# Up projections of a gated feed-forward layer, four tiles at a time, with seven products of token halves for half of the contraction

## The chip, the cores and the metric

The kernel runs on one core of one Trainium2 chip, as one program. The metric is device time of one execution in microseconds (us), the median over several executions. The engines are named as the profile names them: PE is TensorE (PEld its weight loads, which can run under matmuls), DVE is VectorE, ACT is ScalarE, POOL is GpSimd, SP is SyncE, which here issues most of the DMA transfers.

## The reference

Two trunk layers of a diffusion backbone run over 512 latent tokens of width 1024. Each has a mixer (attention and a gated recurrence in the first, a short gated convolution in the second) and then a gated convolutional feed-forward part. All data are float32. The change lies in the feed-forward part and in the computation of the modulation vectors (`mod`), which runs beside it:

```python
D_MODEL, SEQ, DEPTH, D_FF = 1024, 512, 2, 2816

def conv_ffn(h, w_up, conv_w, conv_b, w_down):
    a, val = jnp.split(h @ w_up, 2, axis=-1)
    return (jax.nn.gelu(dwconv3(a, conv_w, conv_b), approximate=False) * val) @ w_down

for layer in range(DEPTH):
    mod = silu_c @ ada_w[layer] + ada_b[layer]
    ...                                   # the mixer of the layer, x = x + gate_m * y
    h = modulate(rms_norm(x, norm_ffn_w[layer]), shift_f, scale_f)
    x = x + gate_f[:, None, :] * conv_ffn(h, ffn_w_up[layer], ffn_conv_w[layer],
                                          ffn_conv_b[layer], ffn_w_down[layer])
```

## The kernel before

Every float32 operand of a large product is split into a hi part in TensorE's rounded format and a lo part that holds the rest, and a product is three matmuls: hi·hi, hi·lo and lo·hi (`mm3`, L246 to L248). Activations lie with features on the 128 partitions and the 512 tokens along a row. So `h` is eight tiles of 128x512 (`src[k]`, a hi and a lo part each, named `hf`), and the up projection makes 44 output tiles of 128x512: 22 for `a` and 22 for `val`.

The class `Weights` feeds the products. A raw tile (`wraw`, two buffers of 1 MB) is loaded by a DMA that SP issues (L59). `conv` makes the hi part of 1024 columns on ACT (L84, `whi`) and the lo part on DVE (L85, `wlo`). Each has three buffers, so a new hi part waits until the matmuls that read the third last one are done.

`ffn_up` goes through eleven steps. Step 0 is `quad`: four tiles at once in two halves of 256 tokens, since the second half of `h` is still being normalised while the first is used (`rest`). Steps 1 to 10 are a pair of `a` tiles (`pair`: two tiles, eight parts of the contraction, three matmuls each, 48 matmuls of 512 columns), then a pair of `val` tiles. Here the two pairs are called a group. Behind a pair the convolution over tokens (`conv3`: one ACT instruction L1079, two DVE instructions L1080 and L1081), the gelu (L1108), the product with `val` (L1116) and the split of the result (L242 on ACT, L243 on DVE) follow, straight out of PSUM. PSUM has six banks for such results (`acc_t`), each of 512 columns.

`units` runs pieces of `mod` between products: one piece is a load of 256 KB (`ar`) and one DVE instruction (L462), and every eighth piece adds some more and a small matmul (`pad`). Before the change layer 0's up projection has 20 pieces, its down projection (`project_back` of `d0`) four per step, and the mixer of layer 1 two per call.

The framework that builds the program takes the instructions of each engine from the code and puts them into an order of its own. Engines run their own instructions in that order and wait for one another by semaphores.

## Time and profile before

| what | before |
|---|---|
| median of three runs (lowest to highest) | 1344.23 us (1342.78 to 1346.13) |
| the profiled execution | 1343.25 us |
| its span, first to last instruction | 1341.5 us |
| granted TensorE clock, mean over the span | 0.999 |
| busy share of PE, DVE, ACT, POOL | 98%, 61%, 39%, 6% |
| HBM traffic | 165.21 MB read, 2.10 MB written |

The profiled execution is 1.75 us longer than its span, and 0.98 us shorter than the median. A busy share is a mean over all stages of the kernel; what one stage is bound by is read from its own stretch.

### The profile page before, as it was taken

To read this page: it belongs to the slowest core of one execution; us is meant where nothing else is said; L and a number is where in the kernel's file an instruction comes from. 1 tells how busy PE (TensorE), PEld (TensorE's weight loads), DVE (VectorE), ACT (ScalarE), POOL (GpSimd) and SP (SyncE) were. 2 spreads that over 40 slices of the span, in tenths; PEclk is the share of its full clock that TensorE was granted. 3 is DMA by queue.
4 is the path that set the end of the run, shared out by engine and by line. 5 is a ranking of instruction groups with operands and counts; after the bars stand their busy time and mean duration, and the time that the engine had idled before them with its cause. 6 is when DMAs were issued, how large, how long until landed. Compare 5 with 4: busy or idle time off the path is not lost. (4 is left out here: it accounts for less than half of the span.)

```text
span 1341.5 us, 19127 instructions
## 1 busy us (share of the span) xinstructions
PE 1318.2 (98%) x7736; PEld 1126.1 (84%) x7736; DVE 821.3 (61%) x1354; ACT 527.9 (39%) x815; POOL 84.4 (6%) x87
## 2 busy tenths in 40 slices
...
GB/s 290 266 125 80 32 32 85 149 188 132 151 196 95 118 118 118 118 118 126 123 205 196 206 95 141 141 144 168 128 95 120 97 100 103 101 99 73 88 110 63
DMA packets 170825, 172.21 MB, mean 128 GB/s; under 512 B 14321, under 2 KB 144753, under 8 KB 170737
## 3 DMA queue, kind: packets, MB, share of 16 engines
...
q8 instruction: 60, 0.98, 0.3%
q14 instruction: 29, 0.23, 0.1%
HBM read 165.21 MB, written 2.10 MB: 125 GB/s over the span
## 5 line engine op out<-in xcount | busy, mean ns | idle before, releaser
L84 ACT CAST whi<-wraw 128x1024 fp32r<-128x1024 f32 (+1 forms) x202 | 207.7, 1031 | 469.2 <-PE ppv L247 93.4
L85 DVE TENSOR_TENSOR wlo<-wraw,whi 128x1024 fp32r<-128x1024 f32 (+1 forms) x202 | 243.5, 1207 | 217.8 <-ACT whi L84 216.5
L247 PE MATMUL ppa<-hf,whi 128*128 128x512 f32 (+1 forms) x448 | 161.6, 361 | 0.0
L246 PE MATMUL ppa<-hf,whi 128*128 128x512 f32 (+1 forms) x448 | 161.2, 360 | 0.0
L248 PE MATMUL ppa<-hf,wlo 128*128 128x512 f32 (+1 forms) x448 | 160.2, 358 | 0.0
L247 PE MATMUL ppv<-hf,whi 128*128 128x512 f32 x320 | 126.1, 394 | 0.0
L246 PE MATMUL ppv<-hf,whi 128*128 128x512 f32 x320 | 125.8, 393 | 0.0
L248 PE MATMUL ppv<-hf,wlo 128*128 128x512 f32 x320 | 124.3, 388 | 0.0
L462 DVE SCALAR_TENSOR_TENSOR aa<-ar,sil,aa 128x512 f32<-128x512 f32 x140 | 105.4, 753 | 17.4 <-DMA ar<-in_ada_w_dram 15.9
L1205 PE MATMUL pd<-whi,g 128*128 128x256 f32 x352 | 98.1, 279 | 0.0
L1207 PE MATMUL pd<-wlo,g 128*128 128x256 f32 x352 | 98.0, 278 | 0.0
L1206 PE MATMUL pd<-whi,g 128*128 128x256 f32 x352 | 97.7, 278 | 0.0
L246 PEld LDWEIGHTS ppa<-hf,whi 128*128 128x128 f32 x448 | 84.1, 188 | 13.9
L248 PEld LDWEIGHTS ppa<-hf,wlo 128*128 128x128 f32 x448 | 84.1, 188 | 13.2
L247 PEld LDWEIGHTS ppa<-hf,whi 128*128 128x128 f32 x448 | 84.2, 188 | 12.2
L1116 DVE TENSOR_TENSOR ppv<-ppv,cv 128x512 f32<-128x512 f32 x40 | 28.0, 700 | 86.0 <-PE ppv L248 86.0
L246 PE MATMUL pbd<-g,whi 128*128 128x512 f32 (+1 forms) x192 | 72.3, 377 | 0.0
L247 PE MATMUL pbd<-g,whi 128*128 128x512 f32 (+1 forms) x192 | 72.0, 375 | 0.0
L248 PE MATMUL pbd<-g,wlo 128*128 128x512 f32 (+1 forms) x192 | 71.7, 373 | 0.0
L246 PEld LDWEIGHTS ppv<-hf,whi 128*128 128x128 f32 x320 | 60.1, 188 | 13.8
L248 PEld LDWEIGHTS ppv<-hf,wlo 128*128 128x128 f32 x320 | 60.1, 188 | 13.4
L247 PEld LDWEIGHTS ppv<-hf,whi 128*128 128x128 f32 x320 | 60.2, 188 | 11.9
...
## 6 DMA issues: line engine op xcount, KB each, us to landing
wraw<-in_ffn_w_up_dram SPq DMA_DIRECT2D x44, 1024.0 KB, 5.1
ar<-in_ada_w_dram SPq DMA_DIRECT2D x160, 256.0 KB, 2.9
wraw<-in_ffn_w_down_dram SPq DMA_DIRECT2D x16, 1024.0 KB, 5.1
wraw<-in_od_w_in_dram SPq DMA_DIRECT2D x12, 1024.0 KB, 5.3
...
wraw<-in_ev_w_out_dram SPq DMA_DIRECT2D x4, 1024.0 KB, 7.3
```

The costliest lines, as they stand in the source:

```text
L84: self.nc.scalar.copy(hv, rv)
L85: self.pin(self.nc.vector.tensor_tensor(lv, rv, hv.bitcast(F32), ALU.subtract))
L246: TE.matmul(o, wh, mh, start=start, stop=False, skip_group_check=True)
L247: TE.matmul(o, wh, ml, start=False, stop=False, skip_group_check=True)
L248: TE.matmul(o, wl, mh, start=False, stop=stop, skip_group_check=True)
L462: pin(V.scalar_tensor_tensor(self.acc[:], raw[:], sil[:, r, 0:1], self.acc[:], ALU.mult, ALU.add))
L1116: V.tensor_tensor(ov[i][:], ov[i][:], t[i][:], ALU.mult)
L1205: TE.matmul(o[i][:, 0:256], gh[:, ts], w[0][:, k - k0], start=k == 0, stop=False)
L1206: TE.matmul(o[i][:, 0:256], gl[:, ts], w[0][:, k - k0], start=False, stop=False)
L1207: TE.matmul(o[i][:, 0:256], gh[:, ts], w[1][:, k - k0], start=False, stop=k == FT - 1)
```

## The change

The up projection's steps 1 to 10 become ten calls of `group`, which makes four tiles at once: two of `a` and two of `val`, in four PSUM banks. The contraction is cut in two. The second half (`k` 4 to 7) is done as before in matmuls of 512 columns (blocks `W1` for the first `a` and `val` tile, `W2` for the second). The first half (`k` 0 to 3) is a product of a 2x2 arrangement of weight blocks with a 2x2 arrangement of inputs (two halves of `k`, two halves of the tokens) by seven products instead of eight, each of 12 matmuls of 256 columns. Its weight blocks are `A11`, `A12`, `A22` and the sums `S1` to `S4`, made by four DVE instructions of 512 columns per group (`_block`); its inputs are quarters of `h` and the differences `T1` to `T4`, made once per layer (`differences`), behind the quad's normalisation. `T1` overwrites a part of `h` that nobody needs after the quad. Partial products that go into more than one output are copied out of PSUM by ACT (eight copies of 256 columns per group) and added by DVE (four of 256, two of 512); the convolution and the rest then read SBUF. The weights come from a new array `upq` in the order of use, two tiles of 1 MB per group as before. The pieces of `mod` leave layer 0's up projection for its down projection (five per step) and for the mixer of layer 1 (three per call); layer 1's up projection has two calls per group for nine groups. The line numbers of the changed code are higher by 4 to some 160: its matmuls are L288 to L290, its hi and lo parts L125 and L126, its copies L1176, its adds L1181 and L1201.

```diff
+QORDER = ["S1", "A11", "A12", "W1", "S2", "S3", "S4", "A22", "W2"]
...
+        nm = self.plan[c][1][s]
+        while self.nload <= min(c + 1 + (nm == "W2"), len(self.plan) - 1):
             self._load()
+        if isinstance(nm, str):
+            self._block(c, nm)
+            return
...
+    HOME = {"S1": ("a", 0), "A11": ("a", 1), "A12": ("b", 0), "W1": ("c", None), "S2": ("d", 0), "S3": ("d", 1),
+            "S4": ("e", 0), "A22": ("e", 1), "W2": ("f", None)}
+    def _block(self, c, nm):
+        V = self.nc.vector
+        quarters = self.raw[c][0]
+        A21, A22, A11, A12 = (quarters[:, 0, 512 * i : 512 * i + 512] for i in range(4))
+        if nm == "S1":
+            s3 = self.pool.tile([P, 512], F32, tag="ws3", name=f"ws3{self.nsub}", bufs=1)
+            V.tensor_tensor(s3[:], A11, A21, ALU.subtract)
+            self.half["S3"] = s3[:]
+            V.tensor_tensor(A21, A21, A22, ALU.add)
+        elif nm == "S2":
+            V.tensor_tensor(A21, A21, A11, ALU.subtract)
+        elif nm == "S4":
+            V.tensor_tensor(A21, A12, A21, ALU.subtract)
+        if nm in ("W1", "W2"):
+            at = 1024 * (nm == "W2")
+            src = self.raw[c + 1][0][:, 0, at : at + 1024]
+        else:
+            src = {"A11": A11, "A12": A12, "A22": A22, "S3": self.half.get("S3")}.get(nm, A21)
+        key, z = self.HOME[nm]
+        if z in (None, 0):
+            self.half[key] = [self.pool.tile([P, 1024], F32R, tag=t, name=f"{t}{self.nsub}", bufs=3) for t in ("whi", "wlo")]
+        at = 512 * (z or 0)
+        hi, lo = (t[:, at : at + src.shape[-1]] for t in self.half[key])
+        self.nc.scalar.copy(hi, src)
+        V.tensor_tensor(lo, src, hi.bitcast(F32), ALU.subtract)
+        self.ready.append(tuple(t.rearrange("p (g k c) -> p g k c", g=2, c=P) for t in (hi, lo)))
+        self.nsub += 1
...
     def ffn_up_plan(l):
-        r = []
-        for j in range(FT // 2):
-            r += cols(up[l], 256 * j) + cols(up[l], FF + 256 * j)
+        r = cols(up[l], 0) + cols(up[l], FF)
+        for j in range(FT // 2 - 1):
+            q = [a["upq"][l, j, i][:, None, :] for i in range(2)]
+            r += [([q[0]], QORDER), ([q[1]], [])]
         return r
...
-                units(4)
+                units(4 if len(groups) == 1 else 5)
...
-    def quad(nm, src, rest):
+    def quad(nm, src, rest, done=lambda: None):
...
+        done()
...
+    def differences(l, src):
+        A, B = HALF
+        h = []
+        for k in range(4):
+            t = gp.tile([P, T], F32, tag=f"g{k}", name=f"hs{l}{k}")
+            V.tensor_tensor(t[:], src[k][0].bitcast(F32), src[k][1].bitcast(F32), ALU.add)
+            h.append(t)
+        d = [gp.tile([P, 2, TC], F32, tag=f"g{4 + i}", name=f"df{l}{i}") for i in range(4)]
+        r = [None] + [fp.tile([P, 2, 2, TC], F32R, tag=f"T{i}", name=f"T{l}{i}") for i in (2, 3, 4)]
+        for z in range(2):
+            V.tensor_tensor(d[0][:, z], h[z][:, B], h[z][:, A], ALU.subtract)
+        for i in (1, 2, 3):
+            for z in range(2):
+                m = h[2 + z][:, A if i == 3 else B]
+                n = {1: d[0][:, z], 2: h[z][:, B], 3: d[1][:, z]}[i]
+                V.tensor_tensor(d[i][:, z], m, n, ALU.subtract)
+            split(r[i][:, 0], r[i][:, 1], d[i][:])
+        quarter = lambda k0, c: lambda z: (src[k0 + z][0][:, c], src[k0 + z][1][:, c])
+        mv = {f"T{i + 1}": (lambda t: lambda z: (t[:, 0, z], t[:, 1, z]))(r[i]) for i in (1, 2, 3)}
+        mv.update({"T1": quarter(0, B), "B11": quarter(0, A), "B21": quarter(2, A), "B22": quarter(2, B),
+                   "X": quarter(4, slice(0, T))})
+        def first():
+            for z in range(2):
+                split(src[z][0][:, B], src[z][1][:, B], d[0][:, z])
+        return mv, first
+    def group(nm, mv):
+        bank = [[acc_t(f"p{m}{g_}{nm}") for g_ in range(2)] for m in range(2)]
+        R = [[fp.tile([P, T], F32, tag=t, name=f"R{nm}{t}{m}", bufs=n) for t, n in ((own, 1), ("t", 5))]
+             for m, own in enumerate(("sqa", "r"))]
+        base = ws.ncall
+        w = {}
+        A, B = HALF
+        def product(m, c, wn, xn, first=False, gs=(0, 1)):
+            while wn not in w:
+                w[QORDER[len(w)]] = ws.get(0)
+            wh, wl = w[wn]
+            nk = wh.shape[2]
+            for g_ in gs:
+                for k in range(nk):
+                    mh, ml = mv[xn](k)
+                    mm3(bank[m][g_][:, c], wh[:, g_, k], wl[:, g_, k], mh, ml, first and k == 0, k == nk - 1)
+        def upto(n):
+            ws.ahead(base + n - ws.ncall)
+        def copy(m, c, r, rc):
+            for g_ in range(2):
+                S.copy(R[r][g_][:, rc], bank[m][g_][:, c])
+        def add(m, c, r, rc):
+            for g_ in range(2):
+                o = R[r][g_][:, rc]
+                V.tensor_tensor(o, bank[m][g_][:, c], o, ALU.add)
+        W = slice(0, T)
+        upto(4)
+        product(0, B, "S1", "T1", True)
+        product(1, A, "A11", "B11", True)
+        copy(0, B, 1, B)
+        upto(6)
+        product(0, A, "A12", "B21")
+        copy(1, A, 0, A)
+        upto(8)
+        product(0, W, "W1", "X", gs=(0,))
+        product(1, A, "S2", "T2")
+        product(0, W, "W1", "X", gs=(1,))
+        copy(1, A, 0, B)
+        upto(9)
+        product(1, A, "S3", "T3")
+        product(0, B, "S4", "B22")
+        add(1, A, 1, B)
+        for g_ in range(2):
+            V.tensor_tensor(R[0][g_][:], bank[0][g_][:], R[0][g_][:], ALU.add)
+        yield R[0]
+        upto(11)
+        product(1, A, "A22", "T4")
+        upto(12)
+        product(1, W, "W2", "X")
+        copy(1, A, 1, A)
+        add(1, B, 1, B)
+        yield R[1]
 
...
     def ffn_up(l, src, rest):
         g = []
...
+        mv = []
+        def gated_tile(f, oa, ov):
+            col = lambda n: fcv[l][:, n : n + 1]
+            tt = fp.tile([P, T], F32, tag="t", name=f"cv{l}{f}", bufs=5)
+            conv3(tt, oa, col(f), col(22 + f), col(44 + f), col(66 + f))
+            S.activation(tt[:], tt[:], AF.Gelu)
+            gh, gl = gtiles(l, f)
+            V.tensor_tensor(ov[:], ov[:], tt[:], ALU.mult)
+            split(gh, gl, ov[:])
+            g.append((gh, gl))
+        def before():
+            rest()
+            mv.extend(differences(l, src))
+        oa, ov = quad(f"a{l}", src, before, lambda: mv[1]())
+        for i in range(2):
+            gated_tile(i, oa[i], ov[i])
+        for j in range(1, FT // 2):
+            for i, (ra, rv) in enumerate(group(f"{l}{j}", mv[0])):
+                gated_tile(2 * j + i, ra, rv)
+            if l and j < 9:
+                units(2)
         return g
...
-            units(2)
+            units(3)

What the order of instructions becomes is shown at three places in the middle of layer 0's groups. In the group shown, `p_5843` and `p_5844` are the banks of the first `a` and `val` tile, `p_5845` and `p_5846` those of the second; `wraw_5734` holds the group's quarter blocks and `wraw_5778` its `W1` and `W2`.

PE before, within a pair: one bank after another, three matmuls per part of the contraction.

```order
L247 MATMUL ppa_5785<-hf_4134,whi_5706 128x512
L248 MATMUL ppa_5785<-hf_4134,wlo_5707 128x512 [waits DVE_49]
L246 MATMUL ppa_5785<-hf_4135,whi_5706 128x512
L247 MATMUL ppa_5785<-hf_4135,whi_5706 128x512
L248 MATMUL ppa_5785<-hf_4135,wlo_5707 128x512
```

PE after, from the end of `A12`'s product for the second bank: `S2` (`whi_5882`, `wlo_5883`) and `W1` (`whi_5851`, `wlo_5852`).

```order
L290 MATMUL p_5844<-hf_4137,wlo_5802 128x256
L288 MATMUL p_5845<-T_4584,whi_5882 128x256 [waits Activation_49]
L289 MATMUL p_5845<-T_4584,whi_5882 128x256
L288 MATMUL p_5844<-hf_4138,whi_5851 128x512
L289 MATMUL p_5844<-hf_4138,whi_5851 128x512
L290 MATMUL p_5844<-hf_4138,wlo_5852 128x512 [waits DVE_49]
L290 MATMUL p_5845<-T_4584,wlo_5883 128x256 [waits DVE_49]
L288 MATMUL p_5845<-T_4584,whi_5882 128x256
L289 MATMUL p_5845<-T_4584,whi_5882 128x256
L288 MATMUL p_5843<-hf_4136,whi_5801 128x256 [waits Activation_49]
```

The matmuls are no longer in the order of one bank: two of `S2` stand behind half of `A12` with a wait for ACT, three of 512 columns from `W1` behind them, then three more of `S2` that wait for DVE, and the other half of `A12`, which waits for ACT.

ACT before, around the same step: hi parts of weights (L84), the first tap (L1079), the gelu (L1108) and hi parts of results (L242).

```order
L1079 ACTIVATE cv_5399<-ppa_5340,vec 128x512 [waits PE_49]
L1108 ACTIVATE cv_5399<-cv_5399 128x512 [waits DVE_49,Activation_49]
L84 CAST whi_5477<-wraw_5333 128x1024 [waits PE_49]
L242 CAST g_5467<-ppv_5414 128x512 [waits DVE_49]
L84 CAST whi_5483<-wraw_5408 128x1024 [waits DMAHW5_49,PE_49]
```

ACT after, from the hi part of `W1` to the hi part of `A22`; `R06` are the group's SBUF copies.

```order
L125 CAST whi_5851<-wraw_5778 128x1024 [waits DMAHW4_49]
L1176 COPY R06t_5850<-p_5844 128x256 [waits PE_49]
L1176 COPY R06sqa_5847<-p_5845 128x256 [waits PE_49]
L125 CAST whi_5882<-wraw_5734 128x512 [waits DVE_49,PE_49]
L125 CAST whi_5882<-ws_5780 128x512
L1235 ACTIVATE cv_5833<-cv_5833 128x512 [waits DVE_49,Activation_49]
L1176 COPY R06r_5849<-p_5843 128x256
L1176 COPY R06t_5848<-p_5846 128x256 [waits PE_49]
L284 CAST g_5838<-R05t_5637 128x512 [waits DVE_49]
L125 CAST whi_5903<-wraw_5734 128x512 [waits PE_49]
```

Behind one hi part of 1024 columns stand copies out of PSUM now, and the hi part of `S2` waits for DVE and for PE. The copy of `p_5843` stands behind both hi parts and a gelu.

DVE before, around a `val` pair: the product with the gate, lo parts of weights and results.

```order
L462 SCALAR_TENSOR_TENSOR aa_5244<-ar_5391,sil,aa_5244 128x512 [waits DMAHW2_49,DVE_49]
L1116 TENSOR_TENSOR ppv_5414<-ppv_5414,cv_5394 128x512 [waits PE_49]
L85 TENSOR_TENSOR wlo_5478<-wraw_5333,whi_5477 128x1024 [waits Activation_49]
L243 TENSOR_TENSOR g_5468<-ppv_5414,g_5467 128x512 [waits Activation_49]
L1116 TENSOR_TENSOR ppv_5415<-ppv_5415,cv_5399 128x512 [waits DVE_49,PE_49]
L85 TENSOR_TENSOR wlo_5484<-wraw_5408,whi_5483 128x1024 [waits DMAHW5_49,Activation_49]
```

DVE after, from the first tap of the group before's second tile to the first add of this group's `S3` product; `R05` and `cv_5833` belong to the group before.

```order
L1213 SCALAR_TENSOR_TENSOR cv_5833<-R05r_5636,vec,cv_5833 128x511 [waits DVE_49]
L126 TENSOR_TENSOR wlo_5852<-wraw_5778,whi_5851 128x1024 [waits DMAHW4_49,Activation_49]
L1214 SCALAR_TENSOR_TENSOR cv_5833<-R05r_5636,vec,cv_5833 128x511 [waits DVE_49]
L126 TENSOR_TENSOR wlo_5883<-wraw_5734,whi_5882 128x512 [waits PE_49,Activation_49]
L126 TENSOR_TENSOR wlo_5883<-ws_5780,whi_5882 128x512 [waits Activation_49]
L1237 TENSOR_TENSOR R05t_5637<-R05t_5637,cv_5833 128x512 [waits Activation_49]
L114 TENSOR_TENSOR wraw_5734<-wraw_5734 128x512 [waits DVE_49]
L285 TENSOR_TENSOR g_5839<-R05t_5637,g_5838 128x512 [waits Activation_49]
L126 TENSOR_TENSOR wlo_5904<-wraw_5734,whi_5903 128x512 [waits PE_49,Activation_49]
L126 TENSOR_TENSOR wlo_5904<-wraw_5734,whi_5903 128x512 [waits Activation_49]
L1181 TENSOR_TENSOR R06r_5849<-p_5845,R06r_5849 128x256 [waits PE_49]
```

Between the lo parts of five blocks now stand a sum of weight blocks (L114), both taps, the gate and the split of the group before; behind them stands an add out of PSUM (L1181) that waits for PE.

## Rows read from the trace of the kernel before

**Rows 1.** The page's first part: busy time of each engine, its share of the span and its instructions.

```profile
PE 1318.2 (98%) x7736; PEld 1126.1 (84%) x7736; DVE 821.3 (61%) x1354; ACT 527.9 (39%) x815; POOL 84.4 (6%) x87
```

**Rows 2.** The timeline of TensorE: the first matmul of the quad of layer 0, the first matmul behind that quad, and the first matmul of two pairs that follow one another. Columns: start and duration in us, engine, line, operation, output<-inputs.

```profile
418.43 0.28 PE L246 MATMUL ppa<-hf,whi 128*128 128x256 f32 x1
441.14 0.39 PE L246 MATMUL ppa<-hf,whi 128*128 128x512 f32 x1
463.35 0.39 PE L246 MATMUL ppa<-hf,whi 128*128 128x512 f32 x1
474.34 0.39 PE L246 MATMUL ppv<-hf,whi 128*128 128x512 f32 x1
```

**Rows 3.** Busy time of each engine in three stretches, number of instructions in brackets, then the granted clock (1.00 is all of it), the DMA share and GB/s: the ten groups of layer 0, the ten groups of layer 1, and the front of layer 0's down projection.

```profile
441.14:661.58 220.44, 220.44 (x969) 180.97 (x968) 122.80 (x161) 82.28 (x108) 0.00 (x0) 1.00 0.39 122
985.98:1206.55 220.57, 220.57 (x970) 181.10 (x969) 117.81 (x150) 82.82 (x108) 0.00 (x0) 1.00 0.33 108
661.58:760.00 98.42, 98.42 (x433) 80.44 (x432) 63.80 (x99) 24.51 (x28) 0.00 (x0) 1.00 0.61 190
```

**Rows 4.** VectorE's groups of instructions, shapes kept apart: count, then busy us and mean ns of one, then the idle time ahead of them and what ended it. L85 is the lo part of weights, L1081 a tap of the convolution, L243 the lo part of an activation, L1212 a 256-column operation out of PSUM in the last projection.

```profile
L85 DVE TENSOR_TENSOR wlo<-wraw,whi 128x1024 fp32r<-128x1024 f32 x190 | 233.0, 1228 | 191.9 <-ACT whi L84 190.6
L1081 DVE SCALAR_TENSOR_TENSOR cv<-ppa,vec,cv 128x511 f32<-128x511 f32 x44 | 32.9, 747 | 1.0
L243 DVE TENSOR_TENSOR g<-ppv,g 128x512 fp32r<-128x512 f32 x40 | 27.4, 684 | 0.0
L1212 DVE TENSOR_TENSOR yt<-pd,gb 128x256 f32<-128x256 f32 x16 | 6.5, 421 | 18.5 <-PE pd L1207 18.5
```

**Rows 5.** ScalarE's groups in the same form (hi parts of 1024 and 512 columns, the first tap of the convolution, a copy of 256 columns out of PSUM, the gelu), and one group of TensorE's weight loads.

```profile
L84 ACT CAST whi<-wraw 128x1024 fp32r<-128x1024 f32 x190 | 198.6, 1048 | 421.9 <-PE ppv L247 92.5 <-PE ppa L247 91.1 <-PE pd L1206 53.7
L84 ACT CAST whi<-wraw 128x512 fp32r<-128x512 f32 x4 | 2.5, 622 | 17.8 <-PE pd L1206 13.1 <-PE pd L1207 4.7
L1079 ACT ACTIVATE cv<-ppa,vec 128x512 f32<-128x512 f32 x44 | 34.1, 775 | 18.0 <-PE ppa L248 18.0
L586 ACT COPY ckt<-pkc 128x256 f32<-128x256 f32 x8 | 3.0, 371 | 28.2 <-PE pkc L584 28.2
L1108 ACT ACTIVATE cv<-cv 128x512 f32<-128x512 f32 x44 | 27.8, 632 | 90.2 <-DVE cv L1081 90.1
L246 PEld LDWEIGHTS ppa<-hf,whi 128*128 128x128 f32 x448 | 84.1, 188 | 13.9
```

**Rows 6.** VectorE's timeline in three places where one instruction follows another: start, duration. The last two rows are a pair in which the second needs the first.

```profile
114.51 0.69 DVE L624 TENSOR_TENSOR qn<-qn,qh 128x512 f32<-128x512 f32 x1
115.11 1.22 DVE L85 TENSOR_TENSOR wlo<-wraw,whi 128x1024 fp32r<-128x1024 f32 x1
116.25 1.22 DVE L579 TENSOR_TENSOR_SCAN qn<-cst,fg 128x512 f32<-128x512 f32 x1
608.60 0.75 DVE L1080 SCALAR_TENSOR_TENSOR cv<-ppa,vec,cv 128x511 f32<-128x511 f32 x1
609.26 0.74 DVE L462 SCALAR_TENSOR_TENSOR aa<-ar,sil,aa 128x512 f32<-128x512 f32 x1
625.08 0.74 DVE L1080 SCALAR_TENSOR_TENSOR cv<-ppa,vec,cv 128x511 f32<-128x511 f32 x1
625.86 0.75 DVE L1081 SCALAR_TENSOR_TENSOR cv<-ppa,vec,cv 128x511 f32<-128x511 f32 x1
```

**Rows 7.** Two hand-overs on the timelines: a matmul of 512 columns and the VectorE instruction that waits for it; a ScalarE copy and the two matmuls behind it, the first of which waits for it.

```profile
507.07 0.39 PE L248 MATMUL ppv<-hf,wlo 128*128 128x512 f32 x1
507.50 0.70 DVE L1116 TENSOR_TENSOR ppv<-ppv,cv 128x512 f32<-128x512 f32 x1 [2.81 <-PE ppv L248]
354.29 0.58 ACT L810 COPY vn<-pvt 128x512 f32<-128x512 f32 x1
354.93 0.50 PE L246 MATMUL pg<-h,whi 128*128 128x512 f32 x1 [1.31 <-ACT vn L810]
355.26 0.40 PE L247 MATMUL pg<-h,whi 128*128 128x512 f32 x1
```

**Rows 8.** DMA issues: output<-input, engine, count, KB each, median us from issue to landing.

```profile
wraw<-in_ffn_w_up_dram SPq DMA_DIRECT2D x44, 1024.0 KB, 5.1
...
wraw<-in_ev_w_out_dram SPq DMA_DIRECT2D x4, 1024.0 KB, 7.3
```

**Rows 9.** VectorE's timeline ahead of the quad of layer 0 (the first matmul of the quad is in rows 2): lo parts of weights (L85), the residual (L960), a sum of squares (L968), the lo part of the first input tile (L990).

```profile
402.97 1.22 DVE L85 TENSOR_TENSOR wlo<-wraw,whi 128x1024 fp32r<-128x1024 f32 x1
408.60 0.75 DVE L960 SCALAR_TENSOR_TENSOR xT<-pbo,mod,xT 128x512 f32<-128x512 f32 x1
411.96 0.43 DVE L968 TENSOR_TENSOR sqaf<-sqaf,sqf 128x256 f32<-128x256 f32 x1 [0.48 <-ACT sqf L965]
415.78 0.48 DVE L960 SCALAR_TENSOR_TENSOR xT<-pbo,mod,xT 128x256 f32<-128x256 f32 x1 [1.66 <-PE pbo L248]
417.69 0.49 DVE L990 SCALAR_TENSOR_TENSOR hf<-uf,mod,hf 128x256 fp32r<-128x256 f32 x1 [0.24 <-ACT hf L986]
```

**Rows 10.** The timelines of ScalarE and VectorE right behind that quad: the convolution's first tap, and its two other taps.

```profile
440.37 0.78 ACT L1079 ACTIVATE cv<-ppa,vec 128x512 f32<-128x512 f32 x1 [8.98 <-PE ppa L248]
441.18 0.75 DVE L1080 SCALAR_TENSOR_TENSOR cv<-ppa,vec,cv 128x511 f32<-128x511 f32 x1 [8.01 <-ACT cv L1079]
441.96 0.75 DVE L1081 SCALAR_TENSOR_TENSOR cv<-ppa,vec,cv 128x511 f32<-128x511 f32 x1
```

36 lines of the change are left out of this document (9 added, 27 removed).

## The prediction

> **What bounds the kernel now.** I read the busy shares first: TensorE is busy 98% of the span, VectorE 61% [rows 1]. Then the stretches of the change: in the ten groups of either layer TensorE is busy for the whole window, 220.44 of 220.44 us and 220.57 of 220.57, at the granted clock 1.00, while VectorE works 122.80 and 117.81 us of it [rows 3]. So these stretches cost what their matmuls cost, and fewer columns bring time as long as no other engine becomes late. Then the pace on TensorE's timeline. The quad's 192 matmuls of 256 columns take 441.14 - 418.43 = 22.71 us, 0.1183 each; a pair's 48 of 512 take 474.34 - 463.35 = 10.99 us, 0.2290 each [rows 2]. Half the columns cost 0.517 of the time.
>
> **What TensorE saves.** A group before: 96 matmuls of 512, 21.98 us. After: 7 x 12 = 84 of 256, 9.94 us, and 48 of 512, 10.99 us, together 20.93. That is 1.05 less, 21.0 over twenty groups. The rest of the sum is what of this is lost to waits.
>
> **A steady group on the other engines.** VectorE's durations are 1.23 (1024 columns), 0.69 (512), 0.75 (a tap) and 0.42 (256) [rows 4]. Back to back, starts follow closer: 0.60 for 512, 1.14 for 1024, 0.66 for a tap [rows 6]; each about 0.08 less than the duration, so I take 0.34 for 256. A tap that needs the one just ahead starts 0.78 behind it [rows 6]; in the order after, another instruction stands between each two taps of a tile. A group has 17 instructions of 512 (four sums of blocks, seven lo parts, two adds, two gates, two splits), two of 1024, four taps and four of 256: 10.2 + 2.28 + 2.64 + 1.36 = 16.5 us of some 21. Before, the same count (four lo parts of 1024, four taps, two gates, two splits) gives 9.6 and what `mod` adds. So VectorE fits by its sum, but with little to spare, and its chain has to be followed.
>
> Two hand-overs. A waiting engine starts 0.04 after a matmul's end (507.07 + 0.39 to 507.50), and a matmul result of 256 columns ends 0.28 after its start [rows 2, 7]. TensorE resumes 0.05 after a copy's end and loses 0.10 more to the weight load (354.87 to 354.93, the next matmul 0.33 behind instead of 0.23) [rows 7]: 0.15.
>
> *The stall at `S2`.* Its hi part goes into the buffer that `A11` had (three buffers, six tiles per group), so it waits for `A11`'s last matmul. From that matmul's start: 0.28 + 0.04 + 0.62 for a hi part of 512 [rows 5] + 0.15 = 1.09. TensorE has this matmul and six of `A12` to run, 7 x 0.118 = 0.83. It waits 0.26, in each group from the second on, 18 of 20 (in the first one other work lies there). Group period 20.93 + 0.26 = 21.19.
>
> *VectorE's ring.* From the first add of `S3`'s product (L1181, the last row of VectorE's order after) to the lo part of the next `S2` it has 21 instructions: four of 256, two of 1024, four taps, eleven of 512. Steps 1.36 + 2.28 + 2.64 + 6.60 = 12.88, with the last at its whole 0.69: 12.97. From there TensorE needs 0.15, three matmuls of `S2`, six of `A12`, twelve of `W1`, one and six of `S2`, nine of `W1` and five of `S3`, then 0.28 + 0.04: 21 x 0.118 + 21 x 0.229 + 0.47 = 7.8. Ring 20.74, under the period by 0.45: VectorE waits a little at that add and TensorE doesn't wait for it. ScalarE's nine hi parts, eight copies, two first taps, two gelus and two splits are 4.3 + 2.1 + 3.0 + 1.6 + 1.3 + 1.2 = 13.5 us by durations [rows 5].
>
> The Trainium skill, page "VectorE: DVE Perf Modes", section "The DRAIN you can't avoid", speaks against this: after each operation the next one does not start until the pipe is empty (the section behind it lets one that is not held start earlier). By that the ring would take whole durations, the second rival below. The rows agree with the earlier start so far, 0.60 for 0.69.
>
> *Copies.* TensorE's order after has waits for ScalarE at the second half of `A12`: half a bank may be written only when the copy of its other half is done. That copy stands behind both hi parts of `S2`'s tile and a gelu. The first of these ends at 23 x 0.118 + 0.94 = 3.66 us of the group; with some 0.09 of overlap each the others end at 4.2 and 4.7 and the copy at 5.02 [rows 5]. TensorE is due there at 5.10. Hidden, nothing; uncovered, up to 0.37 [rows 5] + 0.04 + 0.15 = 0.56 per group. I take nothing. (The Trainium skill, page "PSUM — Partial Sum Buffer", section "PSUM bank collisions raise a hardware error", says that two engines must not be in one bank at once, at disjoint columns too. No run here can show it; by it these waits can't be dropped.)
>
> *Loads.* Two raw tiles of 1 MB per group, as before. The buffer of quarter blocks is free after the lo part of `S4`, at about 8.2 of the group: VectorE makes the lo part of `S2` from 3.7 to 4.4, and behind it six instructions of 512 that wait a little for ScalarE. A load of 1 MB lands 5.1 later [rows 8], at 13.4. ScalarE's next first tap waits for the first bank's add, which ends near 14.9, so a hi part of `A11` that starts by 14.3 makes nothing late. Hidden, with 0.9 to spare. SP issues this load and then that of `W1` and `W2`, which is free at 14.0 and needed at 21.8. Layer 1's pieces of `mod`, one instruction of 0.66 in most groups, stand at the lo parts of `A22` and `S4`, ahead of VectorE's wait of some 4 us for `S3`: nothing.
>
> **What is not steady.**
> - *Start of the quad.* VectorE now makes `S3`, `S1` and two lo parts there, 4 x 0.60 = 2.4. The buffer is free at 402.97 + 1.22, the load lands at 409.3, and VectorE is there at 408.60: it waits 0.7 [rows 8, 9]. The waits of 0.48 and 1.66 that it had absorb some of this [rows 9]. TensorE needs the lo part of the first input, made at 417.69, by its second matmul. Between 0 and all of it, 3.1; I take 1.0 per layer, since the first half of the work has the two waits behind it and one lo part has none. 2.0.
> - *The differences.* Four of 512, eight of 256, three lo parts of 512 and two of 256 are 2.4 + 2.7 + 1.8 + 0.7 = 7.6 us of VectorE. The cover is its wait of 8.01 us behind the quad's inputs [rows 10]: nothing, and up to 1 per layer if the casts between them make it late.
> - *The first group.* `A11`'s bank was the quad's, and now waits for both taps of two tiles. With the quad's end (441.14) as zero, the first tap starts at 0.04 [rows 10]; the order puts the two tiles' taps in turn, so the third ends at 0.04 + 0.66 + 0.66 + 0.75 = 2.1, and TensorE resumes at 2.3. `S1` fills 1.42 and a small matmul of `mod` 0.1. 0.8 per layer, 1.6; before, the next banks were free.
> - *Pieces of `mod`.* Twenty more in the mixer of layer 1 and in layer 0's down projection, 0.66 each on VectorE, which has a third of its time free there, 63.80 of 98.42 us [rows 3]. Their loads (five of 256 KB per step on SP) may delay a weight tile. 0 to 3; I take 1.
>
> **The sum.** -21.0 + 18 x 0.26 (4.7) + 2.0 + 1.6 + 1.0 = -11.7. From the profiled execution's 1343.25: 1331.5. The median of the runs stands 0.98 above that execution: 1332.5, forecast 1332.
>
> **The rivals.**
> - *Everything hidden.* ScalarE's order lets `S2` be ready, and the starts cost nothing: -21.0, 1323. Against it stands the wait of `S2` for a matmul 0.83 ahead, which no row makes shorter. 0.10.
> - *VectorE's ring decides, slower than before.* The mechanism is that its instructions do not overlap in this mixture (PSUM, SBUF, dependent buffers), and each takes its whole duration: 4 x 0.42 + 2 x 1.23 + 4 x 0.75 + 11 x 0.69 = 14.7, ring 22.5, 1.3 over the period, 18 times: +23.6, about 1356. It eats the gain where the ring passes 21.19 + 11.7/18 = 21.84, that is 1.1 more than I count, 0.05 per instruction. For it: 0.42 for 256 is measured, 0.34 is inferred, and a dependent tap steps at 0.78. Against it: the back-to-back rows. 0.13.
> - *A load or a copy is late, no change.* One kind of 1 MB load lands after 7.3 [rows 8]. The quarter blocks would come at 15.5, ScalarE's first tap 1.1 late, VectorE's taps behind it 0.8, and the ring rises to 21.6 to 21.9: 18 x 0.4 to 0.7, 1339 to 1345. The copies at their whole 0.56 give 18 x 0.56 = 10, 1342. About 1343; 0.13.
> - *Seven products save nothing*, since a matmul of 256 can't be shorter than its weight load, 0.188 [rows 5]: 84 x 0.07 x 20 = 117 more, 1450. The quad's 0.1183 with one weight load per matmul speaks against it. 0.01.
>
> **How the numbers follow.** The forecast with its own bounds (starts 0 to 3.1, pieces 0 to 3, the late differences) goes from 1327 to 1339 and has 0.63. A measurement of this kernel tells about 0.3%, 4 us, from no change: faster means below 1340.2, slower above 1348.3. Faster 0.63 + 0.10, less 0.01 for its own tail and with part of the third rival on the edge: 0.72. Same 0.15, slower 0.13. The range must leave out at most 2 in 10: from the first rival's 1323 through the third's, with the lower part of the ring's, 1323 to 1349.
>
> **What would show it.** In the profile after: group period 21.2 us; a wait of the first `S2` matmul for ScalarE's hi part, some 18 times 0.26; VectorE waiting about 4 us per group ahead of L1181 and nowhere long; its starts still 0.60 apart; a wait of `A11` for a tap of L1214 twice, 0.8; waits of 0 to 3 us at the quads' starts; the loads of `upq` landing in about 5 us. I am wrong if TensorE waits for VectorE's lo parts in every group, if L108 waits for its load, or if the 256-column matmuls run slower than 0.12.

## The result and the profile after

The changed kernel takes 1334.22 us (median of four runs, 1333.44 to 1334.61), beside 1344.56 us before in the same comparison. The ratio is 0.9923, with a 95% interval of 0.9906 to 0.9940: 10.3 us faster. The forecast was 1332, with a range of 1323 to 1349. The profiled execution took 1333.99 us, with a span of 1332.2, 9.3 less than before. A second comparison of the same kernel, shown below, gave a ratio of 0.9943 (0.9930 to 0.9957).

The page after, in its first part and its row on the loads of the new array:

```profile
PE 1304.5 (98%) x8456; PEld 1147.6 (86%) x8456; DVE 965.4 (72%) x1688; ACT 625.2 (47%) x1085; POOL 84.3 (6%) x87
...
wraw<-in_upq_dram SPq DMA_DIRECT2D x40, 1024.0 KB, 4.8
```

TensorE has 13.7 us less to do than in [rows 1], VectorE 144 more and ScalarE 97 more. A load of the new array lands 4.8 us after its issue, where one of 1 MB took 5.1 [rows 8].

The busy time by stretch in the trace after (the ten groups of layer 0, those of layer 1, and layer 0's down projection; columns as in [rows 3]):

```profile
441.10:652.46 211.36, 210.75 (x1325) 189.94 (x1323) 169.63 (x275) 126.85 (x235) 0.00 (x0) 1.00 0.29 102
985.00:1197.25 212.25, 211.51 (x1330) 190.45 (x1329) 178.19 (x292) 127.18 (x235) 0.00 (x0) 1.00 0.32 110
652.46:783.63 131.17, 127.45 (x591) 105.20 (x590) 90.39 (x140) 36.39 (x45) 0.00 (x0) 0.97 0.66 212
```

and the down projection before, whole:

```profile
661.58:785.01 123.43, 123.43 (x589) 102.93 (x588) 79.59 (x121) 35.30 (x43) 0.00 (x0) 1.00 0.63 200
```

The groups fell from 220.44 to 211.36 us and from 220.57 to 212.25, together by 17.4. The down projection of layer 0, whose matmuls the change doesn't touch, rose from 123.43 to 131.17, by 7.7. All the rest differs by 0.4 in sum, nearly all of it in the mixer and the quad of layer 1: -17.4 + 7.7 + 0.4 = -9.3, the difference of the spans. In the last row TensorE was idle for 131.17 - 127.45 = 3.7 us, and its busy time itself is 4.0 us longer, at a mean granted clock of 0.97.

TensorE's timeline after: the first matmul of the quad, of the first, second, third and fourth group of layer 0, and of the down projection.

```profile
418.35 0.28 PE L288 MATMUL ppa<-hf,whi 128*128 128x256 f32 x1
441.10 0.28 PE L288 MATMUL p<-hf,whi 128*128 128x256 f32 x1
462.80 0.28 PE L288 MATMUL p<-hf,whi 128*128 128x256 f32 x1
483.80 0.28 PE L288 MATMUL p<-hf,whi 128*128 128x256 f32 x1
504.88 0.28 PE L288 MATMUL p<-hf,whi 128*128 128x256 f32 x1
652.46 0.39 PE L288 MATMUL pbd<-g,whi 128*128 128x512 f32 x1
```

The quad takes 441.10 - 418.35 = 22.75, where it took 22.71 [rows 2]. The first group takes 21.70, and from the third on a group takes 21.08. Those of layer 1 take 21.08 to 21.44, the first 21.74. So two things ask for a reason: where the down projection's 7.7 us come from, which the forecast didn't have, and whether the 0.15 us between the period of 21.08 and TensorE's 20.93 is the wait that the forecast names.

### The profile page after: what moved, and what is told of

Its sections match the earlier page's. It is cut to its first block, busy times and chain, and to the rows that moved or that the text cites. A ratio compares the mean times of both kernels' runs of the same rounds, so it can differ in the third digit from the quotient of the medians.

```text
span 1332.2 us, 21229 instructions
## 1 busy us (share of the span) xinstructions
PE 1304.5 (98%) x8456; PEld 1147.6 (86%) x8456; DVE 965.4 (72%) x1688; ACT 625.2 (47%) x1085; POOL 84.3 (6%) x87
## 5 line engine op out<-in xcount | busy, mean ns | idle before, releaser
L92 ACT CAST whi<-wraw 128x1024 fp32r<-128x1024 f32 (+1 forms) x122 | 124.1, 1021 | 280.8 <-PE pd L1340 70.4
L93 DVE TENSOR_TENSOR wlo<-wraw,whi 128x1024 fp32r<-128x1024 f32 (+1 forms) x122 | 145.2, 1192 | 107.7 <-ACT whi L92 107.1
L288 PE MATMUL p<-hf,whi 128*128 128x512 f32 (+1 forms) x640 | 215.4, 338 | 1.4 <-ACT whi L125 1.4
L290 PE MATMUL p<-hf,wlo 128*128 128x512 f32 (+1 forms) x640 | 214.6, 335 | 0.0
L289 PE MATMUL p<-hf,whi 128*128 128x512 f32 (+1 forms) x640 | 214.1, 335 | 0.0
L125 ACT CAST whi<-wraw 128x512 fp32r<-128x512 f32 (+1 forms) x160 | 113.0, 727 | 85.0 <-PE p L289 35.0
L290 PEld LDWEIGHTS p<-hf,wlo 128*128 128x128 f32 x640 | 120.1, 188 | 13.6
L288 PEld LDWEIGHTS p<-hf,whi 128*128 128x128 f32 x640 | 120.1, 188 | 12.3 <-ACT whi L125 1.6
L289 PEld LDWEIGHTS p<-hf,whi 128*128 128x128 f32 x640 | 120.1, 188 | 10.7
L126 DVE TENSOR_TENSOR wlo<-wraw,whi 128x512 fp32r<-128x512 f32 (+1 forms) x160 | 128.1, 817 | 0.9 <-ACT whi L125 0.5
L504 DVE SCALAR_TENSOR_TENSOR aa<-ar,sil,aa 128x512 f32<-128x512 f32 x140 | 104.8, 749 | 24.1 <-DMA ar<-in_ada_w_dram 21.8
L288 PE MATMUL pbd<-g,whi 128*128 128x512 f32 (+1 forms) x192 | 73.5, 383 | 0.0
L289 PE MATMUL pbd<-g,whi 128*128 128x512 f32 (+1 forms) x192 | 73.3, 382 | 0.0
L290 PE MATMUL pbd<-g,wlo 128*128 128x512 f32 (+1 forms) x192 | 73.1, 381 | 0.0
L288 PE MATMUL p<-T,whi 128*128 128x256 f32 x240 | 69.0, 288 | 0.0
L290 PE MATMUL p<-T,wlo 128*128 128x256 f32 x240 | 67.2, 280 | 0.0
L289 PE MATMUL p<-T,whi 128*128 128x256 f32 x240 | 67.2, 280 | 0.0
L1340 PEld LDWEIGHTS pd<-whi,g 128*128 128x128 f32 x352 | 66.3, 188 | 0.0
L1339 PEld LDWEIGHTS pd<-whi,g 128*128 128x128 f32 x352 | 66.1, 188 | 0.0
## 6 DMA issues: line engine op xcount, KB each, us to landing
wraw<-in_upq_dram SPq DMA_DIRECT2D x40, 1024.0 KB, 4.8
wraw<-in_ffn_w_down_dram SPq DMA_DIRECT2D x16, 1024.0 KB, 5.3
wraw<-in_od_w_in_dram SPq DMA_DIRECT2D x12, 1024.0 KB, 5.6
wraw<-in_ev_w_out_dram SPq DMA_DIRECT2D x4, 1024.0 KB, 6.9
```

The lines of the kernel that those rows point to most:

```text
L92: self.nc.scalar.copy(hv, rv)
L93: self.pin(self.nc.vector.tensor_tensor(lv, rv, hv.bitcast(F32), ALU.subtract))
L125: self.nc.scalar.copy(hi, src)
L126: V.tensor_tensor(lo, src, hi.bitcast(F32), ALU.subtract)
L288: TE.matmul(o, wh, mh, start=start, stop=False, skip_group_check=True)
L289: TE.matmul(o, wh, ml, start=False, stop=False, skip_group_check=True)
```

## The experiments

**The pieces of `mod` back between the groups.** The down projection lost time with more pieces of `mod` in it. The first run takes them out again.

```diff
-                units(4 if len(groups) == 1 else 5)
+                units(4)
...
             if l and j < 9:
                 units(2)
+            if not l:
+                units(2 if j == 1 else 1)
```

> The changed kernel, with the pieces of mod that its down projection of layer 0 got put back between the groups of layer 0: four per step again instead of five, and one per group (two in the first). My theory: these pieces cost 7.7 us in the down projection, since the pieces' loads come late there, TensorE's small matmul waits for VectorE twice (1.91 and 1.82 us) and its granted clock falls behind each wait; in the groups VectorE has 4.2 us free ahead of L1181, so they cost nothing there. The down projection goes from 131.2 back to about 123.6, the group period stays 21.1, and the time is 1334.2 - 7.6 = about 1326.5 (1325.5 to 1328). Rival 1: the down projection is longer because of what the groups leave behind for VectorE and ScalarE at its start; then it stays near 131 and the time at 1334. Rival 2: VectorE's ring in the groups has no room for 0.66 more; then the period rises to about 21.5 and the time is about 1330.

Measured: 1329.14 us (1326.82 to 1331.91), ratio 0.9895 (0.9880 to 0.9910). The down projection of layer 0 in its trace:

```profile
652.64:776.08 123.44, 123.44 (x590) 102.94 (x589) 78.84 (x121) 36.21 (x45) 0.00 (x0) 1.00 0.61 197
```

That is the time before the change, with the idle time and the slow clock both gone. The groups of layer 0 took 211.77, 0.4 more than in the changed kernel. Layer 1's took 1.0 us more, for one group of 22.27 us, in which VectorE waited for the next quarter blocks:

```profile
1016.09 0.69 DVE L108 TENSOR_TENSOR ws<-wraw 128x512 f32<-128x512 f32 x1 [1.53 <-DMA wraw<-in_upq_dram]
```

The pieces caused the loss, and the groups have room for them. The profiled execution took 1327.51 us, one of the two shorter ones of this kernel; the two others took 3.3 and 4.4 us more, and without their traces it stays open whether late loads are the whole of that. It was run once more beside another kernel:

> The same kernel as the run that put the pieces back between layer 0's groups, beside the one with the pieces inside the groups on the same chip: 1327 to 1331 if its spread is its own, with one or two groups of 22 us or more in its profile.

Measured: 1328.70 us (1328.17 to 1329.27), ratio 0.9889 (0.9872 to 0.9905). No group was over 21.83 us in this profile. So whether a group is late differs from execution to execution.

**The pieces without their loads.** VectorE may be late there because of its work, or because of what it waits for. In the changed kernel's trace, VectorE in the down projection, at the last piece but one ahead of a reduction and at the reduction (the last piece stands between the two rows):

```profile
666.11 0.75 DVE L504 SCALAR_TENSOR_TENSOR aa<-ar,sil,aa 128x512 f32<-128x512 f32 x1 [2.94 <-DMA ar<-in_ada_w_dram]
667.69 0.71 DVE L508 TRANSPOSE_TENSOR_REDUCE ad<-aa 128x16 f32<-128x512 f32 x1
```

and TensorE, at the small matmul that needs this reduction, the matmuls behind it, and the second such place:

```profile
668.45 0.40 PE L514 MATMUL pad<-ad,cst 128*128 128x16 f32 x2 [1.91 <-DVE ad L508]
669.80 0.63 PE L288 MATMUL pbd<-g,whi 128*128 128x512 f32 x1
670.23 0.63 PE L289 MATMUL pbd<-g,whi 128*128 128x512 f32 x1
...
702.07 0.36 PE L514 MATMUL pad<-ad,cst 128*128 128x16 f32 x2 [1.82 <-DVE ad L508]
```

VectorE waited 2.94 us for a load of 256 KB, so the reduction ended at 668.40 and TensorE stood for 1.91 us. In the matmuls behind it, from 669.38 us on, the starts are 0.43 apart, where they were 0.229 [rows 2]. The granted clock in two stretches right behind the two waits (it is the third number from the end):

```profile
668.50:672.50 4.00, 4.00 (x12) 3.17 (x13) 3.86 (x9) 0.00 (x0) 0.00 (x0) 0.57 0.61 204
702.50:706.80 4.30, 4.30 (x13) 3.35 (x13) 3.24 (x7) 1.04 (x1) 0.00 (x0) 0.60 0.76 223
```

At 0.57 and 0.60 the engine spent most of these 4.0 and 4.3 us at the lower of its two levels, 1.2 GHz. Behind the wait of 0.61 us in the first group (below) no start is 0.43 apart. The expectations count on such a fall behind each of these waits; two profiles further down show that it doesn't always come.

The next run leaves out the loads of these pieces and keeps VectorE's instructions, so `mod` isn't computed there.

```diff
     def load(self):
         ...
+        if self.fixed:
+            self.raw[n] = self.raw[n - 1]
+            return
         raw = ap_.tile([P, T], F32, tag="araw", name=f"ar{n}", bufs=3)
...
         for n, (mp_, gi) in enumerate(steps):
+            ada.fixed = nm == "d0" and n < len(steps) - 1
```

> The changed kernel in which the pieces of mod in layer 0's down projection read a tile that is there already: their 55 loads of 256 KB are left out there (so mod is not computed), VectorE's instructions stay all 55. Theory: VectorE is late there because it waits for these loads (15.2 us in 12 waits), not because of its work; without them the small matmuls find their operand ready, TensorE doesn't wait, its clock stays at 1.00 and the down projection takes 123.5 to 124 instead of 131.2: 1326 to 1327. Rival: VectorE's work is too much (55 x 0.66 more than the hi and lo parts leave room for); then the waits stay and the time is 1332 to 1334.

Measured: 1328.70 us (1326.84 to 1329.56), ratio 0.9886 (0.9871 to 0.9902). The down projection:

```profile
653.61:777.83 124.22, 124.07 (x592) 103.02 (x590) 90.14 (x140) 36.42 (x45) 0.00 (x0) 1.00 0.34 109
```

VectorE has the same busy time as in the changed kernel (90.14 and 90.39 us), and the loss is gone but for 0.8. So the loads make it late, not the work. The profiled execution took 1329.56 us and not the 1326 to 1327 expected: one group of layer 1 took 22.39 us, 1.3 over its neighbours, for a late load of quarter blocks, and layer 0's quad began at 419.36 us, 1.0 later than in the changed kernel.

**The pieces moved in the kernel before.** The opposite test: the old up projection, and the pieces where the change puts them.

```diff
-                units(4)
+                units(4 if len(groups) == 1 else 5)
...
-                units(1 + l)
+                units(2 * l)
...
-            units(2)
+            units(3)
```

> The kernel before, with the pieces of mod moved as the change moves them and nothing else: none in layer 0's up projection, five per step in its down projection, three per call in layer 1's mixer, four per pair of pairs in layer 1. Theory: the loss in the down projection comes from the pieces alone, so it takes 131 instead of 123.4 there too, and the time is about 1344 + 7.7 = 1351.5. Rival: the groups' end (adds and taps left over for VectorE, another order of loads) makes VectorE late; then the down projection stays at 123.4 and the time at 1344.

Measured: 1348.32 us, between 1345.00 and 1350.76 in ten runs, ratio 1.0029 (1.0017 to 1.0042). Its down projection, and the one wait of TensorE in it:

```profile
662.10:788.25 126.15, 124.35 (x593) 103.12 (x592) 89.52 (x141) 35.26 (x43) 0.00 (x0) 1.00 0.68 218
```

```profile
708.26 0.37 PE L472 MATMUL pad<-ad,cst 128*128 128x16 f32 x2 [1.80 <-DVE ad L466]
```

The pieces alone make the old kernel slower, by 3.9 (by the ratio) and not by 7.7. The profiled execution had one of the two waits, 1.80 us long, and lost 2.7 us in the down projection. Behind this wait the granted clock stayed at 1.00, and TensorE made 20 matmuls in 4.0 us, where the changed kernel made 12 behind its first wait:

```profile
708.50:712.50 4.00, 4.00 (x20) 3.29 (x20) 3.41 (x8) 1.05 (x1) 0.00 (x0) 1.00 0.72 210
```

The other executions left no trace, but their mean granted clock is on record: 0.998 to 0.999 in the three shortest (1345.00 to 1346.76 us), 0.996 in the three longest (1350.37 to 1350.76). That would fit none to two waits, with or without a lower clock behind them, but is no proof of it. So the cause is settled, and its size here only in part: in the profiled execution one of the two waits was missing, and so was the lower clock behind the other. Why, I did not separate.

The run answers another question too. Its ten groups of layer 0, still of the old form, took 219.89 us, 0.55 less than before. So the moved pieces account for some 0.5 of the 9.1 us that these groups gained; the rest comes with the new product.

**The small matmul called later.** If only TensorE's wait in the small matmul harms, it is enough to call that later.

```diff
-            self.late += [(self.calls + 3, gather), (self.calls + 5, finish)]
+            self.late += [(self.calls + 5, gather), (self.calls + 7, finish)]
```

> The changed kernel with its pieces of mod where the change put them, but the small matmul that TensorE waits in (L514) is called two pieces later, five behind its reduction instead of three. Theory: VectorE's lateness in the down projection harms only through that matmul: TensorE stands in it for 1.8 to 1.9 us, and its granted clock falls behind the wait. Two pieces later its operand is ready, TensorE doesn't wait, the clock stays, and the down projection falls from 131.2 to 123.5 to 124.5: 1326.5 to 1327.5. Rival: the pieces make VectorE's lo parts late too, or the matmul just waits further down; then a wait for VectorE stays in the down projection and the time is 1330 to 1334.

Measured: 1331.26 us (1331.18 to 1331.56), ratio 0.9914 (0.9899 to 0.9929). The down projection fell as expected:

```profile
655.89:780.97 125.08, 124.54 (x592) 103.20 (x590) 90.08 (x140) 36.18 (x45) 0.00 (x0) 1.00 0.68 221
```

but the time by 3.0, half of it (by the ratios of the two comparisons only 1.2), since the edit holds in the whole program: the attention part ended 2.7 us later (its output projection starts at 365.67 us, in the changed kernel at 362.96). So it was made again for the down projection alone, beside the changed kernel itself.

```diff
-            self.late += [(self.calls + 3, gather), (self.calls + 5, finish)]
+            self.late += [(self.calls + 3 + self.more, gather), (self.calls + 5 + self.more, finish)]
...
+            ada.more = 2 if nm == "d0" and n < len(steps) - 1 else 0
```

> The changed kernel with the small matmul of the pieces called two pieces later in layer 0's down projection alone, and everywhere else where it was. With it later everywhere the down projection took 125.08 instead of 131.17, and the attention part ahead of the change lost 2.7. Theory: without that loss the rest of the gain shows: the down projection takes 125 and the time is 1334.2 - 6 = about 1328 (1327.5 to 1329). Rival: the 125.08 there was the luck of that profile, since VectorE's lateness varies; then a wait of about 1.8 for VectorE stays and the time is 1331 to 1334.

> The changed kernel itself again, on the chip of the run with the later small matmul: 1333.5 to 1334.7, with two waits of about 1.8 us for VectorE in the down projection, and the down projection 131 us. If its waits come and go, as the kernel before with the pieces moved showed them (one in its profile, times over 5.8 us), then 1330 to 1334.5.

Measured: 1329.34 us (1327.13 to 1330.56), ratio 0.9893 (0.9880 to 0.9907), against 1336.46 us (1333.92 to 1338.13), ratio 0.9943 (0.9930 to 0.9957), for the changed kernel on the same chip: 7.1 us apart. The down projection of the first, and the two waits of the second:

```profile
653.22:777.53 124.31, 124.14 (x592) 103.28 (x590) 89.98 (x140) 36.16 (x45) 0.00 (x0) 1.00 0.68 223
```

```profile
668.47 0.40 PE L514 MATMUL pad<-ad,cst 128*128 128x16 f32 x2 [1.87 <-DVE ad L508]
701.78 0.58 PE L514 MATMUL pad<-ad,cst 128*128 128x16 f32 x2 [3.09 <-DVE ad L508]
```

With all 55 pieces in place and VectorE as busy as ever, the down projection takes 124.31 us at the full granted clock. In the repeated run one of the waits was 3.09 us long, the down projection took 132.05, and two groups of layer 1 took 22.4 and 22.8. So all but 0.9 of the 7.7 us is TensorE's standing in this matmul and the lower clock behind it.

How much of it is the clock differs. The stretches behind the repeated run's two waits:

```profile
668.50:672.50 4.00, 4.00 (x19) 3.33 (x20) 3.86 (x9) 0.00 (x0) 0.00 (x0) 1.00 0.66 201
702.00:708.00 6.00, 6.00 (x16) 4.77 (x17) 3.52 (x8) 1.05 (x1) 0.00 (x0) 0.52 0.65 193
```

Behind 1.87 us of standing, at the same place where 1.91 had been followed by 0.57, the clock stayed at 1.00; behind 3.09 us it was 0.52 over 6.0 us.

**Another table of buffers.** The first wait in the forecast's sum is that of `S2`'s hi part for `A11`'s buffer. In the trace after, TensorE's last matmul of `A12`'s first half and the first two of `S2`:

```profile
550.46 0.28 PE L290 MATMUL p<-hf,wlo 128*128 128x256 f32 x1
550.63 0.38 PE L288 MATMUL p<-T,whi 128*128 128x256 f32 x1
550.85 0.28 PE L289 MATMUL p<-T,whi 128*128 128x256 f32 x1
```

The starts are 0.17 and 0.22 apart instead of 0.118: 0.05 of waiting and 0.10 for the weight load, 0.15 together, in every group. The run takes that wait away.

```diff
-    HOME = {"S1": ("a", 0), "A11": ("a", 1), "A12": ("b", 0), "W1": ("c", None), "S2": ("d", 0), "S3": ("d", 1),
+    HOME = {"S1": ("a", 0), "A11": ("b", 0), "A12": ("b", 1), "W1": ("c", None), "S2": ("d", 0), "S3": ("d", 1),
```

> The changed kernel with one line of its table of buffers changed: S1 has a buffer of its own, A11 shares one with A12 (which had half a buffer empty). So the hi part of S2 waits for S1's last matmul instead of A11's. My theory: the period of 21.08 is TensorE's 20.93 and the wait of the first S2 matmul, 0.15; it falls to 20.93 to 20.97 and 18 groups give 2.0 to 2.7 us: 1331.5 to 1332.2. Rival 1: VectorE's ring sets the period (21.08 is near the ring of 20.74 as I counted it); then the period stays at 21.08 and the time at 1334.2. Rival 2: the hi part of A11, which must now wait for A22's last matmul, makes S1 and the first tap late and the period rises to 21.3 or more: 1338.

Measured: 1338.09 us (1336.85 to 1339.58), ratio 0.9961 (0.9949 to 0.9973): slower than the change, by 2.4 to 5.1 us by the ratios of the change's two comparisons. TensorE's timeline: a wait in its first group, and in a later one the step from `S2`'s last matmul to the second half of `A12`:

```profile
446.03 0.36 PE L288 MATMUL p<-hf,whi 128*128 128x256 f32 x1 [0.98 <-DVE cv L1214]
...
554.33 0.28 PE L288 MATMUL p<-T,whi 128*128 128x256 f32 x1
554.49 0.39 PE L288 MATMUL p<-hf,whi 128*128 128x256 f32 x1
554.71 0.28 PE L289 MATMUL p<-hf,whi 128*128 128x256 f32 x1
```

None of the three theories: the period is 21.06, so the wait of `S2` did go, and 0.02 was won. Its place was taken by the next one, that of `A12`'s second half for ScalarE's copy (0.16 and 0.22 apart), which the forecast had put at 5.02 against 5.10 us and called hidden. The loss comes from elsewhere. The first groups took 23.6 instead of 21.7, since `A11`, `A12` and the taps now stand in another order and TensorE waits twice for a tap; and the waits in the down projection were 5.1 us in sum in this profile.

Both edits together:

> Both edits together: pieces of mod back between the groups of layer 0, and the other table of buffers. If both theories hold, their gains add: 1334.2 - 7.6 - 2.4 = about 1324 (1323 to 1326). If VectorE's ring gets the period once TensorE's wait is gone and a piece of 0.66 stands in the ring as well, the period stays near 21.1 and the time is 1326 to 1328.

Measured: 1332.75 us (1331.01 to 1334.20), ratio 0.9921 (0.9907 to 0.9934). They don't add: the first groups are 23.6 again, the down projection 123.75, and a late load made one group of 22.35. The run with the pieces alone is better.

**Three more instructions for VectorE.** VectorE waits for 4.2 us in each group after, just ahead of the add that starts its ring (and the steps that the forecast counted with are there: 0.60 between starts at 0.68 of duration, 0.34 at 0.42). The last row is TensorE's, its first matmul that reads the lo part of `S2`:

```profile
550.61 0.69 DVE L126 TENSOR_TENSOR wlo<-wraw,whi 128x512 fp32r<-128x512 f32 x1
559.30 0.42 DVE L1181 TENSOR_TENSOR R06r<-p,R06r 128x256 f32<-128x256 f32 x1 [4.21 <-PE p L290]
...
560.77 0.42 DVE L1181 TENSOR_TENSOR R06t<-p,R06t 128x256 f32<-128x256 f32 x1
561.11 0.68 DVE L1201 TENSOR_TENSOR R06sqa<-p,R06sqa 128x512 f32<-128x512 f32 x1
561.71 0.68 DVE L1201 TENSOR_TENSOR R06t<-p,R06t 128x512 f32<-128x512 f32 x1
...
551.66 0.28 PE L290 MATMUL p<-T,wlo 128*128 128x256 f32 x1
```

The lo part of `S2` ends at 551.30, and TensorE needs it at 551.66, so with the hand-over some 0.3 us are to spare, whatever the wait of 4.2 says. The run puts 1.8 us into the ring.

```diff
-        V.tensor_tensor(lo, src, hi.bitcast(F32), ALU.subtract)
+        for _ in range(4 if nm == "A12" else 1):
+            V.tensor_tensor(lo, src, hi.bitcast(F32), ALU.subtract)
```

> The changed kernel in which the lo part of A12 is made four times in each group: three more VectorE instructions of 512, 3 x 0.60 = 1.8 us per group, at a place where TensorE needs the result only a microsecond later. It measures VectorE's ring. By the forecast's count the ring is 20.74 with TensorE's part in it, so it becomes 22.54 and sets the period: 22.5 instead of 21.08 in 18 groups, about +26 us, 1360. Rival: VectorE has 4.2 us of waiting per group ahead of L1181 in the profile, so 1.8 more fit and the period and the time stay, 1334.

Measured: 1356.25 us (two runs, 1356.11 and 1356.39), ratio 1.0092 (1.0072 to 1.0112). The period is 21.67, between the two. The first groups are 27.9 and 28.9, 13 us of the 22 in sum. In a steady group, TensorE at the second half of `A12`:

```profile
538.11 0.40 PE L290 MATMUL p<-hf,whi 128*128 128x512 f32 x1
538.97 0.39 PE L289 MATMUL p<-hf,whi 128*128 128x256 f32 x1 [0.46 <-ACT R05r L1177]
```

The framework made another order of it: the lo part of `S3` stands ahead of that of `S2`, and TensorE now waits for a copy out of PSUM that stands behind a gelu on ScalarE, which waits for VectorE's tap. So it was not a clean measurement of the ring, since the order is not fixed. It shows that of 1.8 us more a third comes through to the end, although VectorE still waits, now in two pieces of 1.09 and 2.08 us.

**The pieces behind the quarter blocks' load.** The late group in the first experiment asked what makes a load late.

```diff
-    def group(nm, mv):
+    def group(nm, mv, n_units):
...
         copy(1, A, 0, B)
+        units(n_units)
         upto(9)
...
-            if l and j < 9:
-                units(2)
```

> As the run that put the pieces of mod back between layer 0's groups, but in both layers the pieces are called inside a group, ahead of S3's product, so that VectorE runs them behind the lo part of S4 and SP issues their loads of 256 KB behind the load of the quarter blocks, not ahead of it. In that run the profile shows the quarter blocks late in a group of layer 1 (VectorE waited 1.53 us for them, the period was 22.27 instead of 21.1) and its times spread over 5 us. Theory: the quarter blocks come late because the pieces' loads go ahead of them; behind them there is no such group, the time falls by 0 to 3 us against that run and the times lie closer together: 1326 to 1328. Rival 1: the late load has nothing to do with the pieces' loads (another transfer, or the memory itself); then late groups stay and the time is 1328 to 1330. Rival 2: the pieces' instruction, now just ahead of the add of S3's product, delays it and with it VectorE's ring: the period rises to 21.3 or more and the time to 1330 or more.

Measured: 1328.85 us (1327.71 to 1330.84), ratio 0.9890 (0.9875 to 0.9905), the same as the run beside it. In its trace the quarter blocks were late in one place per layer, in the first group (VectorE), so that the second one took 22.9 and 23.2 us (TensorE waits for a copy). The rows of layer 0:

```profile
459.55 0.69 DVE L108 TENSOR_TENSOR ws<-wraw 128x512 f32<-128x512 f32 x1 [2.07 <-DMA wraw<-in_upq_dram]
```

```profile
467.29 0.39 PE L288 MATMUL p<-hf,whi 128*128 128x256 f32 x1 [1.00 <-ACT R02t L1176]
```

The first groups took 21.8, and all from the third on 21.07 to 21.44. A last run took the pieces out of the first groups; its edit is shown against the run just told. (Its expectation calls the long groups the first ones; the rows show that the load is late in the first and the time is lost in the second.)

```diff
-2 * (j < 10) if l else 1 + (j == 1)
+2 * (j > 1) if l else (0, 0, 2, 2)[j] if j < 4 else 1
```

> As the run with the pieces inside the groups, but the first group of each layer has none (its two are spread over the second and third in layer 0; layer 1 uses groups two to ten). In that run the first group of both layers took 22.9 and 23.2 us instead of 21.7, since VectorE waited 2.1 us for the next quarter blocks, and no other group was late. Theory: the first group is the one whose quarter blocks are loaded while the pieces' first loads start, so without pieces there both fall back to 21.7: 1328.85 - 2.7 = about 1326 (1325.5 to 1327.5). Rival: the first groups are late there because of the order that the framework made around the quad; then they stay at 22.9 or more, or the second group takes it over, and the time is 1328 to 1330.

Measured: 1328.44 us (1327.03 to 1329.33), ratio 0.9890 (0.9874 to 0.9907). The second groups are 21.0 again, as the theory had it, but in layer 1 the third took 22.6, behind a wait of VectorE of 0.60 us for its quarter blocks, and the median did not move. Groups were late only where pieces of `mod` run beside them. In six profiles with no pieces in layer 0's groups (the changed kernel twice, the run without loads, the two with a later small matmul, the other table) no group of layer 0 from the second on took over 21.1. That the loads of 256 KB are what delays the quarter blocks is argued from this; no run separates it. Which load goes late differs between two profiles of the same kernel (none in the changed kernel's first, two groups in its second), and no order of calls here is shown to keep all of them in time.

## Why the prediction was right, and which of its steps were not

- **What bounds it, and what TensorE saves**: right. 20.93 per group was the count, 21.08 is the period, and the 0.15 between is a wait that was in the sum. The pace of 256 columns held, at 0.118 between starts.
- **The stall at `S2`**: right in place, 0.26 forecast, 0.15 measured, so 18 groups lost 2.7 instead of 4.7. ScalarE began that hi part at 549.95, where the last matmul that reads `A11`'s hi part ended at 549.92. That is the second of its three, one earlier than I had counted. The profile names a lo part of VectorE that ended at 549.93 as the releaser, so which of the two it was stays open.
- **VectorE's ring**: the count was good. The steps are 0.60 and 0.34, VectorE waits 4.21 us where some 4 were forecast, and the slack is 0.3 where 0.45 was counted. With whole durations instead of these steps, the way of the second rival, the ring would have been 22.5 and the kernel slower than before. The Trainium skill (page "VectorE: DVE Perf Modes", section "The DRAIN you can't avoid") says that the next operation doesn't start until the pipe is empty, and adds in the same section that one that is not held starts earlier. The trace agrees with the earlier start for these instructions, 0.60 at 0.68, as the rows before did. What the ring would do with more work in it wasn't measured cleanly.
- **Copies**: hidden, but only just. Once the other wait was gone, this one was there with almost the same 0.15.
- **Loads in the groups**: right in the profiled execution (4.8 us, no late group), and the rival's mechanism is real: in other executions and versions a load of quarter blocks came up to 2.1 us late, and a group then took 22.3 to 23.2.
- **Start of the quad**: 2.0 forecast, 0.1 measured (the quads took 22.75 and 22.81 us instead of 22.71, and layer 0's began 0.1 earlier). VectorE's instructions there in the trace after, and in the last row the same load in layer 1:

```profile
408.07 0.69 DVE L108 TENSOR_TENSOR ws<-wraw 128x512 f32<-128x512 f32 x1 [0.23 <-DMA wraw<-in_upq_dram]
411.47 0.68 DVE L110 TENSOR_TENSOR wraw<-wraw 128x512 f32<-128x512 f32 x1
...
415.69 0.48 DVE L1002 SCALAR_TENSOR_TENSOR xT<-pbo,mod,xT 128x256 f32<-128x256 f32 x1 [1.50 <-PE pbo L290]
...
951.04 0.69 DVE L108 TENSOR_TENSOR ws<-wraw 128x512 f32<-128x512 f32 x1 [1.17 <-DMA wraw<-in_upq_dram]
```

  The load was 0.23 late, not 0.7. The sum for `S1` (L110) starts where VectorE had waited 0.48 us before, and the next long wait, for TensorE, fell from 1.66 to 1.50 us [rows 9]: the work went into time in which VectorE waited anyway. I had named this cover and then charged a part of the work all the same. In layer 1 the load was 1.17 late, and the stretch from the down projection's end to the quad, with ten more pieces in it, was only 0.3 longer. "L108 waits for its load" was one of the forecast's signs of being wrong; here it waited, and hardly anything was lost by it.
- **The first group**: 0.8 forecast, 21.70 - 20.93 = 0.77 measured. The wait is where it was put, at `A11`:

```profile
442.46 0.29 PE L514 MATMUL pad<-ad,cst 128*128 128x16 f32 x2
443.36 0.36 PE L288 MATMUL p<-hf,whi 128*128 128x256 f32 x1 [0.61 <-ACT whi L125]
```

  The profile names ScalarE as the releaser here. The tap that I had named ends at 443.2, which fits the matmul's start at 443.36 as well.
- **Pieces of `mod`**: this step failed. "0 to 3; I take 1" was 7.7 in the down projection. I had priced the pieces by VectorE's free time, and VectorE was not short of it; their loads I had counted only as something that may delay a weight tile. What I left out is that a piece waits for its own load, and who waits for the piece: the small matmul stands in TensorE's own queue, so a late load of 256 KB stops TensorE. The kernel before already showed VectorE waiting there for `ar` loads:

```profile
675.26 0.75 DVE L462 SCALAR_TENSOR_TENSOR aa<-ar,sil,aa 128x512 f32<-128x512 f32 x1 [1.50 <-DMA ar<-in_ada_w_dram]
```

  In the changed kernel's first profile the two waits, 3.7 us, cost about 7 with the lower clock behind them. Waits of 1.87 and 1.80 us in two other profiles had no lower clock behind them, so the price of one such wait lies between its length and about twice that.
- **The range**: the forecast's own bounds, added up from its terms (starts 0 to 3.1 per layer, pieces 0 to 3, differences up to 1 per layer), give 1329.5 to 1340.7 for the median, not 1327 to 1339. The measured time lies in both.

That the sum came out so near the time is in part luck, since two errors went opposite ways: 4 us too much for `S2` and the quads, 7 too little for the pieces. What was right by its mechanism is the gain in the groups: 21.0 less 4.7 and 1.6, 14.7 us by the sum, 17.4 measured. The likeliest case held as a whole, but its parts were not as sure as the total looks.

Faster than both kernels is the change with the pieces put back between the groups, or with its small matmul called later in the down projection alone: ratios of 0.9889 to 0.9895 in three comparisons, 14 to 15 us under the kernel before and 5 to 7 under the change.
